# The low parts of the experts' weights made on VectorE alone, instead of on VectorE and GpSimd, in a decoder layer with 32 experts

## The chip, the cores and the metric

The kernel runs on one core of one Trainium2 chip. The metric is the time of one execution on the device in microseconds (us). Engines are named as the profile names them: PE is TensorE's matmul and PEld its weight load, DVE is VectorE, ACT is ScalarE, POOL is GpSimd, SP is SyncE, which here only issues transfers.

## What is computed

One decoder layer over 1024 tokens of width 1024 in float32: a mixer of three branches, a layer norm, then a mixture of experts, and a second layer norm. The change lies in the mixture of experts. Each token takes its 4 best of 32 experts:

```
gu   = x @ w_gu[e] + b_gu[e]                 # 1024 -> 512, gate and up
act  = (clip(up, -7, 7) + 1) * (min(gate, 7) * sigmoid(1.702 * min(gate, 7)))
y   += weight * (act @ w_down[e] + b_down[e])   # 256 -> 1024
```

An expert's weights come as six tiles of 128 x 1024 numbers, 512 KB each: four of `w_gu` (two row blocks of 128 in each) and two of `w_down`.

## The kernel before, in words

**Three products for one.** PE multiplies in a rounded form of float32. To keep the accuracy, every operand is split in two: the high part is a copy in the rounded form (made on ACT), the low part is what the copy lost, operand minus high part (a subtract, `tensor_tensor`, on DVE or POOL). Each product is then three matmuls: high by high, high by low, low by high (`mm3`, lines 221 to 224). `split` (line 217) makes both parts; for the `w_gu` tiles `expert_split` (line 1216) does, with the copy at line 1223 and the subtract at line 1226.

**The experts' loop** (lines 1658 to 1717) goes over 46 blocks of at most 128 rows each. `PLAN` gives each of 32 slots a number of rows; the fullest expert has four blocks, eleven slots have two, twenty have one, the last four of these 64 rows. `ORDER` puts a slot with two blocks between two with one block from the fourth slot on: a triple of three experts has four blocks. In one turn of the loop, for block b, the engines are given in this order: a gather of the rows of block b + 3 (an indirect DMA, issued by POOL, line 1282), the gate-up product of block b in three pieces (`gu_mm`), between them the transposes of block b + 1 (`x_T`) and of the activations of block b - 1 (`act_T`), the activation of block b (`swiglu`, DVE and ACT), the down product of block b - 1 (`down`, whose results DVE scales into the tile `o` at line 1482), and a scatter that adds block b - 2 into the output (an indirect DMA, issued by POOL, line 1488). Each engine works off its own instructions in the order in which they are written.

**The next expert's weights.** While an expert's blocks run, the six weight tiles of the next expert are split. `expert_units` (line 1230) makes six small functions, and `pump` calls them at three places of a turn: after the first third of `gu_mm`, after its last third, and after `down`. With one block in the expert that runs, each place takes two of the six; with two blocks, one. Which engine makes a low part stands in the tuple `engs`, one entry per tile, four for `w_gu` and two for `w_down`. The tuple that is used depends on the blocks of the expert whose weights are split.

**The loads.** The raw tiles lie in a ring of nine places (`mring`). SP issues the six loads of an expert (lines 830 and 833), three experts ahead in the program, but a load waits until the low part of the tile that had its place is made (`mring.give`, line 1227). SP's queue is in order: one load that waits holds all behind it, among them the small loads of the row tables (`table_load`, line 1265), which the gathers wait for.

**Ahead of the loop** the first two experts' weights are split under tuples of their own (line 1252). The second one's four `w_gu` tiles are split by hand (lines 1604 to 1632: two low parts on DVE, two on POOL), so only its last two entries, for `w_down`, are read from its tuple (line 1655).

Of the kernel before, what the change touches and what calls it, by code (L numbers as in the profile page):

```python
# [144 lines left out]
def body(ctx, tc, A, out, offs, dbg=None):  # L145
    nc = tc.nc
    V, G, SC, PE, SY = nc.vector, nc.gpsimd, nc.scalar, nc.tensor, nc.sync
# [51 lines left out]
    def slot(kind, shape, dt=F32):  # L199
        n = turn[kind] = turn.get(kind, -1) + 1  # L200
        tag = SLOTS[kind][n % len(SLOTS[kind])]
        full = [shape[0], 2048 if tag[0] == "r" else 1024] if kind in ("x", "o", "xT", "gu") else None
        pool = keep if kind == "tt" else bigp if tag == "big" else mb[0] if kind in ("sg", "up", "gs") or tag[:2] == "dn" else ph
        if full and len(shape) > 2:
            full = [shape[0], shape[1], full[1] // shape[1]]
        return pool.tile(shape, dt, tag=tag, name=kind, bufs=COUNT.get(tag, 1), padded_shape=full)
# [10 lines left out]
    def split(src, hi, lo, eng=V):  # L217
        SC.copy(hi, src)  # L218
        eng.tensor_tensor(lo, src, hi.bitcast(F32), op=ALU.subtract)  # L219
# [983 lines left out]
    nblk = [-(-n // P) for n in PLAN]  # L1203
# [8 lines left out]
    def expert_loads(s):  # L1212
        for q in range(6):
            mring.add(expert_load(s, q), (s, q))

    def expert_split(s, q):
        r = mring.take((s, q))
        hi_, lo_ = slot("gu", [P, D], F32R), slot("gu", [P, D], F32R)
        for k in range(2):
            ew[s]["gu"][2 * q + k] = (hi_[:, half_of(k)], lo_[:, half_of(k)])  # L1220

        def hi():
            SC.copy(hi_, r)  # L1223

        def lo(eng=V):
            eng.tensor_tensor(lo_, r, hi_.bitcast(F32), op=ALU.subtract)  # L1226
            mring.give((s, q))
        return hi, lo

    def expert_units(s, engs=None):  # L1230
        engs = engs or ((V, V, V, G, G, G) if nblk[s] > 1 else (V, V, V, G, V, G))
        def gu_unit(q):
            def f():
                hi, lo = expert_split(s, q)
                hi()
                lo(engs[q])
            return f

        def dn_unit(k):
            def f():  # L1240
                r = mring.take((s, 4 + k))
                w = slot("dn", [P, 2, D], F32R)
                split(r, w[:, 0, :], w[:, 1, :], engs[4 + k])
                mring.give((s, 4 + k))
                ew[s]["dn"][k] = w
            return f
        return [gu_unit(q) for q in range(4)] + [dn_unit(k) for k in range(2)]

    e0, e1, e2, e3 = order[:4]
    for s in (e0, e1, e2, e3):  # L1250
        expert_loads(s)
    units = [expert_units(e0, (V, V, V, G, V, V)), expert_units(e1, (V, V, G, G, G, G))]

    bgu = slot("bgu", [2 * E, 2 * F], F32R)
    bgf = slot("bgu", [2 * E, 2 * F])
# [402 lines left out]
    for b in range(2, NB + 1):  # L1658
        if b < NB:
            s, i = blocks[b]  # L1660
            if b in (3, 4, 5):
                ovl = next(ovl_steps)
            if b == 5 or b > 5 and i == 0:
                at = 1 if b == 5 else order.index(s)
                for f in pend:
                    f()
                pend = []
                if at > 1 and at + 3 < NS:
                    table_load(order[at + 3])
                    expert_loads(order[at + 3])  # L1670
                if at + 1 < NS:
                    pend = expert_units(order[at + 1])
# [174 lines left out]
```

## Time and profile before

| what | value |
|---|---|
| median of 3 runs | 1115.52 us (1114.58 to 1115.7) |
| the profiled execution | 1116.49 us |
| its span, first to last instruction | 1114.5 us |
| PE busy | 975.9 us, 88% of the span |
| ACT busy | 490.5 us, 44% |
| mean granted clock of TensorE | 0.948 |
| moved by DMA | 219.20 MB, 197 GB/s over the span |

The span is 2 us shorter than the profiled execution's own time, which is 1 us above the median of the other runs. A share of busy time is an average over stages; the experts' loop is a stretch of some 480 us of the span. A granted clock of 1.00 is 2.4 GHz throughout a stretch; 0.91 means that part of it ran at the lower level, 1.2 GHz.

### The profile page before, as it was taken

The page shows a single profiled execution, that of the slowest core. Times are in us where ns is not written, and L with a number is a line of the kernel's source. Part 1 is how long each engine was busy: PE and PEld are TensorE (multiplying, and loading weights), DVE is VectorE, ACT ScalarE, POOL GpSimd, SP SyncE. Part 2 cuts the span into 40 slices and gives each one's busy share as a digit, 9 for nine tenths or more (in the row PEclk, how much of TensorE's full clock was granted, in tenths as well). Part 3 has the DMA queues.
Part 4 walks back from the last instruction along what each step waited for, and adds up shares of the span by engine and source line. Part 5 has one row for each costly group of instructions (what it writes and reads, how often), then busy time and mean ns, then how long its engine had stood idle before and what let it go on. Part 6 is the DMA issues. An engine that isn't in the chain of part 4 may idle for free. (4 is left out here: it accounts for less than half of the span.)

```text
span 1114.5 us, 14260 instructions
## 1 busy us (share of the span) xinstructions
PE 975.9 (88%) x4538; PEld 748.3 (67%) x4538; DVE 852.6 (77%) x1400; ACT 490.5 (44%) x790; POOL 529.3 (47%) x327
## 2 busy tenths in 40 slices
PE   5899999999999988799779999998878989898730
PEld 4678779788887767678657777776655666565420
DVE  5737577836687896577686889998867999989948
ACT  2353132312454443234542546555444664564525
POOL 2540011011001155666682677676575876858633
PEclk9999999999999999799899999999998999999875
DMA  9902247435341236025748899998979899979745
GB/s 311 330 17 78 74 135 225 146 127 192 111 139 48 78 113 200 38 100 172 256 178 226 248 276 317 296 259 250 261 211 289 239 300 280 276 229 297 220 118 207
DMA packets 115652, 219.20 MB, mean 197 GB/s; under 512 B 21166, under 2 KB 42680, under 8 KB 115576
## 3 DMA queue, kind: packets, MB, share of 16 engines
q1 hardware_dynamic: 99416, 181.50, 48.8%
q0 software_dynamic: 16160, 36.78, 14.7%
q8 instruction: 36, 0.59, 0.2%
q14 instruction: 40, 0.33, 0.1%
HBM read 187.27 MB, written 36.78 MB: 201 GB/s over the span
## 5 line engine op out<-in xcount | busy, mean ns | idle before, releaser
L1226 DVE TENSOR_TENSOR gu<-raw,gu 128x1024 fp32r<-128x1024 f32 x95 | 216.8, 2298 | 18.8 <-ACT gu L1223 18.7
L1223 ACT CAST gu<-raw 128x1024 fp32r<-128x1024 f32 x128 | 130.4, 1048 | 47.0 <-DMA raw<-in_w_gu 46.3
L1488 POOL DMA_INDIRECT y_d<-o,tt x46 | 92.3, 2007 | 99.3 <-DVE aT L219 21.2
L223 PE MATMUL bank<-gu,xT 128*128 128x512 f32 (+10 forms) x280 | 111.2, 397 | 12.2 <-POOL gu L1226 10.0
L222 PE MATMUL bank<-gu,xT 128*128 128x512 f32 (+10 forms) x280 | 120.1, 429 | 0.0
L219 POOL TENSOR_TENSOR dn<-raw,dn 128x1024 fp32r<-128x1024 f32 x42 | 116.0, 2899 | 0.5 <-ACT dn L218 0.4
L224 PE MATMUL bank<-gu,xT 128*128 128x512 f32 (+10 forms) x280 | 111.3, 398 | 0.0
L224 PE MATMUL bank<-dn,aT 128*128 128x512 f32 (+11 forms) x184 | 77.8, 423 | 23.3 <-DVE aT L219 23.2
L1282 POOL DMA_INDIRECT x<-h_d,tt x46 | 70.9, 1540 | 53.3 <-DMA raw<-in_w_down 22.1
L1226 POOL TENSOR_TENSOR gu<-raw,gu 128x1024 fp32r<-128x1024 f32 x33 | 81.9, 2483 | 17.5 <-ACT gu L1223 16.9
L222 PE MATMUL bank<-u,w 128*128 128x512 f32 x216 | 86.6, 401 | 0.0
L223 PE MATMUL bank<-u,w 128*128 128x512 f32 x216 | 84.8, 393 | 0.3 <-DVE u L219 0.3
L224 PE MATMUL bank<-u,w 128*128 128x512 f32 x216 | 84.8, 392 | 0.0
L218 ACT CAST dn<-raw 128x1024 fp32r<-128x1024 f32 x64 | 65.3, 1046 | 43.1 <-PE bank L224 24.7
L218 ACT CAST xT<-bank 128x512 fp32r<-128x512 f32 (+11 forms) x92 | 46.4, 507 | 77.0 <-PE bank L1394 73.8
L222 PE MATMUL bank<-w,u 128*128 128x512 f32 (+1 forms) x192 | 76.0, 396 | 3.0 <-ACT u L379 3.0
L222 PE MATMUL bank<-dn,aT 128*128 128x512 f32 (+11 forms) x184 | 77.3, 420 | 0.5 <-ACT aT L218 0.4
L223 PE MATMUL bank<-dn,aT 128*128 128x512 f32 (+11 forms) x184 | 76.5, 416 | 0.0
L335 DVE SCALAR_TENSOR_TENSOR acc<-raw,cact,acc 128x512 f32<-128x512 f32 x80 | 68.0, 850 | 7.7 <-DMA raw<-in_w_ada 5.8
L224 PE MATMUL bank<-w,u 128*128 128x512 f32 (+1 forms) x192 | 70.7, 368 | 2.5 <-POOL u L380 2.4
L1482 DVE SCALAR_TENSOR_TENSOR o<-bank,tt,u 128x512 f32<-128x512 f32 (+11 forms) x92 | 65.4, 740 | 8.1 <-PE bank L224 7.5
L223 PE MATMUL bank<-w,u 128*128 128x512 f32 (+1 forms) x192 | 70.3, 366 | 1.1 <-DVE w L219 1.1
(417 smaller groups left out, 2298.4 us busy)
## 6 DMA issues: line engine op xcount, KB each, us to landing
raw<-in_w_gu SPq DMA_DIRECT2D x128, 512.0 KB
raw<-in_w_down SPq DMA_DIRECT2D x64, 512.0 KB
raw<-in_w_ada SPq DMA_DIRECT2D x32, 512.0 KB
raw<-in_w_ada SPq DMA_DIRECT2D x32, 256.0 KB
raw<-in_w_in SPq DMA_DIRECT2D x12, 512.0 KB
raw<-in_w_out SPq DMA_DIRECT2D x8, 512.0 KB
raw<-in_x SPq DMA_DIRECT2D x8, 512.0 KB
h_d<-h SPq DMA_DIRECT2D x8, 512.0 KB
```

Source lines behind the costliest of these rows:

```text
L218: SC.copy(hi, src)
L219: eng.tensor_tensor(lo, src, hi.bitcast(F32), op=ALU.subtract)
L222: PE.matmul(o, lh, rh, start=first, stop=False)
L223: PE.matmul(o, lh, rl, start=False, stop=False)
L224: PE.matmul(o, ll, rh, start=False, stop=last)
L335: V.scalar_tensor_tensor(acc, w[:, k, :], cact[:, kk:kk + 1], acc, op0=ALU.mult, op1=ALU.add)
L1223: SC.copy(hi_, r)
L1226: eng.tensor_tensor(lo_, r, hi_.bitcast(F32), op=ALU.subtract)
L1282: G.indirect_dma_start(out=x[:n], out_offset=None, in_=src, in_offset=bass.IndirectOffsetOnAxis(ap=segs[blocks[b]][:n, 0:1], axis=0), boun ...
L1482: V.scalar_tensor_tensor(o[:n, half_of(hf)], p_[:n], segs[s, i].bitcast(F32)[:n, 1:2], G2[:n, half_of(hf)], op0=ALU.mult, op1=ALU.mult)
L1488: G.indirect_dma_start(out=y_d, out_offset=bass.IndirectOffsetOnAxis(ap=segs[blocks[b]][:n, 0:1], axis=0), in_=outs.pop(b)[:n], in_offset= ...
```

## The change

Two tuples are replaced. In the loop every one of the six low parts of an expert is now made on DVE; before, POOL made three of six for experts with two blocks and two of six for those with one. Ahead of the loop the two `w_down` tiles of the second expert move to DVE as well. The first expert's tuple keeps one POOL entry, and the two subtracts of lines 1631 and 1632 stay on POOL.

```diff
     def expert_units(s, engs=None):
-        engs = engs or ((V, V, V, G, G, G) if nblk[s] > 1 else (V, V, V, G, V, G))
+        engs = engs or (V,) * 6
...
-    units = [expert_units(e0, (V, V, V, G, V, V)), expert_units(e1, (V, V, G, G, G, G))]
+    units = [expert_units(e0, (V, V, V, G, V, V)), expert_units(e1, (V, V, G, G, V, V))]
```

## Rows read from the trace of the kernel before

**Rows 1.** Page, part 1; groups by line, whole span (busy us, mean ns | idle).
```profile
PE 975.9 (88%) x4538; PEld 748.3 (67%) x4538; DVE 852.6 (77%) x1400; ACT 490.5 (44%) x790; POOL 529.3 (47%) x327
...
L1226 DVE TENSOR_TENSOR gu<-raw,gu 128x1024 fp32r<-128x1024 f32 x95 | 216.8, 2298 | 18.8 <-ACT gu L1223 18.7
...
L219 DVE TENSOR_TENSOR dn<-raw,dn 128x1024 fp32r<-128x1024 f32 x22 | 38.2, 1739 | 2.6 <-ACT dn L218 2.6
```

**Rows 2.** Windows: us, PE PEld DVE ACT POOL busy (x), clock, DMA share, GB/s.
```profile
619.70:669.80 50.10, 47.72 (x227) 36.83 (x226) 43.04 (x48) 26.53 (x39) 35.70 (x18) 1.00 0.95 270
669.80:712.10 42.30, 40.32 (x190) 30.30 (x189) 39.34 (x44) 24.39 (x36) 32.19 (x15) 1.00 0.99 311
754.60:804.30 49.70, 43.78 (x188) 31.80 (x187) 40.88 (x46) 25.11 (x35) 31.60 (x15) 0.93 0.91 258
804.30:860.80 56.50, 44.35 (x188) 30.82 (x187) 38.85 (x42) 24.72 (x35) 35.26 (x17) 0.91 0.83 245
860.80:901.50 40.70, 38.22 (x172) 26.62 (x170) 38.84 (x45) 24.47 (x36) 27.19 (x13) 0.96 0.87 256
901.50:945.20 43.70, 40.37 (x182) 27.65 (x182) 41.79 (x45) 24.33 (x37) 32.00 (x16) 0.96 0.98 289
...
619.70:1032.70 413.00, 373.96 (x1679) 266.26 (x1678) 364.16 (x399) 222.44 (x318) 291.17 (x138) 0.96 0.92 269
```

**Rows 3.** The costliest groups of the loop, 619.7 to 1032.7 us: DVE, then POOL.
```profile
L1226 DVE TENSOR_TENSOR gu<-raw,gu 128x1024 fp32r<-128x1024 f32 x81 | 192.7, 2394 | 18.0 <-ACT gu L1223 17.9
...
L219 DVE TENSOR_TENSOR dn<-raw,dn 128x1024 fp32r<-128x1024 f32 x18 | 28.5, 1582 | 2.6 <-ACT dn L218 2.6
...
L219 POOL TENSOR_TENSOR dn<-raw,dn 128x1024 fp32r<-128x1024 f32 x37 | 102.9, 2935 | 0.0
...
L1226 POOL TENSOR_TENSOR gu<-raw,gu 128x1024 fp32r<-128x1024 f32 x27 | 66.6, 2465 | 8.4 <-ACT gu L1223 7.8
```

**Rows 4.** Lines 1226 and 219, whole span: ns min/median/max, first and last start.
```profile
L1226 DVE TENSOR_TENSOR gu<-raw,gu x95: 1201/1223/6476, 502.1 to 1053.7; 128x1024 fp32r<-128x1024 f32 x95
...
L219 DVE TENSOR_TENSOR dn<-raw,dn x22: 1206/1225/4207, 559.7 to 1059.8; 128x1024 fp32r<-128x1024 f32 x22
```

**Rows 5.** Timeline at 876 us: start us, us, engine line, operation.
```profile
876.36 2.96 POOL L219 TENSOR_TENSOR dn<-raw,dn 128x1024 fp32r<-128x1024 f32 x1
...
876.82 3.59 DVE L1226 TENSOR_TENSOR gu<-raw,gu 128x1024 fp32r<-128x1024 f32 x1
```

**Rows 6.** Waits, 619.7 to 1032.7 us: who <- for whom: us, times, longest.
```profile
ACT gu L1223 <- DMA raw<-in_w_gu: 42.2, 28, 5.6
PE bank L224 <- DVE aT L219: 17.9, 10, 5.1
PE bank L223 <- POOL gu L1226: 10.0, 3, 5.0
...
SPq L830 <- POOL dn L219: 139.7, 37, 10.3
SPq L830 <- POOL gu L1226: 58.5, 18, 12.0
```

**Rows 7.** Timeline at 746 to 764 us: ACT, POOL, SP's queue, PE [idle before <-releaser].
```profile
746.16 1.04 ACT L1223 CAST gu<-raw 128x1024 fp32r<-128x1024 f32 x1 [4.18 <-DMA raw<-in_w_gu]
...
760.60 1.05 POOL L1282 DMA_INDIRECT x<-h_d,tt  x1 [7.75 <-PE bank L1394]
761.68 2.35 POOL L1226 TENSOR_TENSOR gu<-raw,gu 128x1024 fp32r<-128x1024 f32 x1
...
764.06 5.35 SPq L830 DMA_DIRECT2D raw<-in_w_gu  x3
...
764.09 0.50 PE L223 MATMUL bank<-gu,xT 128*124 128x512 f32 x1 [2.96 <-POOL gu L1226]
```

**Rows 8.** Lines 1282 (gathers) and 1488 (scatters): ns min/median/max, first and last start.
```profile
L1282 POOL DMA_INDIRECT x<-h_d,tt x46: 995/1800/2169, 536.3 to 1030.1; - x46
...
L1488 POOL DMA_INDIRECT y_d<-o,tt x46: 1417/1831/5019, 591.9 to 1073.0; - x46
```

## The prediction, made before the changed kernel was run

> **What bounds the kernel now.** I read the page first, for the shares: PE is busiest, DVE next, POOL under half [rows 1]. These are averages, so I cut the experts' loop into stretches by the copy that opens every third expert, from the fourth on; each stretch holds a triple of experts [rows 2]. Between the second and third shown lies one of 42.5 us, much like the second; after the last shown follow two of 43.8 and 43.7. The first stretch works off five blocks, the other eight four each. See three things there. The stretch from 669.8 and the next are full: PE is busy 40.3 of 42.3 us and the transfers take 0.99 of their engines' time. The stretches from 754.6 and 804.3 take 49.7 and 56.5 us for the same work; in them PE idles 5.9 and 12.2 us, its granted clock falls to 0.93 and 0.91, and the transfers fall to 0.91 and 0.83. And over all nine PE idles 39 of 413 us. So PE and the weight loads set the pace where all goes well, and something breaks the flow elsewhere.
>
> Next, the costliest groups of the loop [rows 3]. A low part on DVE takes 2.39 us in the mean, but 1.22 us in the median and 1.20 at least [rows 4]. The timeline says where the rest comes from: DVE's subtract that starts at 876.82, while POOL's runs, ends 1.1 us after POOL's end at 879.32, as if it had begun only then [rows 5]. In the nine stretches 40 of DVE's 99 low parts took over 1.3 us; all 40 lie over a subtract of POOL's, and none of the 59 others took over 1.23 us, though 29 of them lie over a gather or a scatter and no subtract of POOL's. So DVE's busy time holds much standing still behind POOL's subtracts.
>
> Last, the waits [rows 6]. SP's load issues wait 139.7 and 58.5 us for low parts made on POOL; ACT's copies wait 42.2 us for weights that have not landed; PE waits 17.9 us for the low part of the activations (DVE) and 10.0 us for POOL's `w_gu` parts. One place shows how they hang together [rows 7]: a tile's copy ends at 747.2, but POOL stands in a gather that waits 7.75 us for PE's transposes, so the low part runs from 761.68 to 764.03, 14.5 us late. At 764.06 SP can issue the next loads, and at 764.09 PE goes on.
>
> **The change, part by part.**
>
> Moved in the nine stretches: 37 and 27 subtracts, 64, leave POOL [rows 3]; at the median of 1.223 us they add 64 x 1.223 = 78.3 us to DVE. What DVE loses is its standing still: 81 x (2.394 - 1.223) = 94.9 us and 18 x (1.582 - 1.225) = 6.4 us, together 101.3. So DVE goes from 364.2 us to 341, or 37.9 a stretch, against 42.3 in the best full stretch. That leaves room, if not much. If none of the stall were POOL's doing, DVE would need 364.2 + 78.3 = 442.5; these are the two ends. I take the lower one, since all 40 long cases lie over POOL's subtracts.
>
> POOL loses 102.9 + 66.6 = 169.5 us and keeps the gathers and scatters. These now come earlier and meet more subtracts of DVE's. A gather took 1.0 us at least and 1.8 in the median, a scatter 1.4 and 1.8 [rows 8]. Nearest price of meeting one: up to the 0.8 us between a gather's ends; for 74 of them 59 us at most on an engine with 291 - 169 = 122 us of work in 413. Nothing, covered by POOL's idle time; without that cover a gather is 0.8 us late, three blocks before PE needs it.
>
> SP's loads no longer pass POOL's queue. They wait for DVE's low part instead, which stands in DVE's order one place behind the copy of its tile. For the case of rows 7 that would be some 1.3 us after the copy's end, not 14.5. Behind a waiting load stand the row tables that gathers need, so they gain too.
>
> A new wait: DVE's queue now holds the low parts of `w_down` in front of the next turn's transposes and activations. They follow ACT's copy, 1.04 us as in [rows 7], which must follow PE's down product. ACT is ahead of DVE in most turns, and a subtract that waits costs at most that copy. I cost it in the first rival.
>
> One rule of the Trainium skill speaks against the change. Perfetto Trace Analysis, Optimizing Scalar/DVE Operations, says that when DVE is saturated, work may be worth giving to ScalarE or even GPSIMD, with the reserve that GPSIMD shares an SBUF port with DVE. By the first half alone the loop's DVE, 364 of 413 us busy, should get slower by what it is given back; by the reserve the busy time is partly POOL's. The trace agrees with the reserve: 101 us of stall against 78 of work.
>
> **The sum.** What stall goes, the loads and PE are next: even without it no stretch runs faster than PE's work, and the loads at 0.99 as in the best stretch need 0.92 x 413 / 0.99 = 384 us for all nine. So I let each four-block stretch run like the best full ones, at 42.4: 49.7 gives 7.3, 56.5 gives 14.1, the three of 43.7 to 43.8 give 1.3 each (4.0). The five-block one (PE idle 2.4 of 50.1), the two full ones and that of 40.7 I leave. Together 25.4, so 413 becomes 388, close to the 384 of the loads. Outside the nine stretches eight more subtracts move: 8 x 1.22 = 9.8 us more work. The stall there is the whole span's less the nine stretches': 95 x 1.075 - 94.9 = 7.2 us for `w_gu` [rows 1], by the same step 4.9 for `w_down` (22 with a mean of 1.739 [rows 1]). The net is 2.3 less, nearly all in the last experts; I take 2. The sum is 27.4. The profiled execution took 1116.5 (span 1114.5 and 2 around it), so 1089.1; it lies 1.0 above the median, so 1088.
>
> **The rivals.**
>
> DVE becomes the bound in the one-block turns. DVE's 341 us less 163 low parts x 1.223 leave 142 us for 37 blocks, 3.8 each. A one-block turn needs 6 x 1.22 + 3.8 = 11.2 us of DVE against 374 / 37 = 10.1 of PE. For it: two such turns follow each other in each triple. Against it: the two-block expert has 5 us to catch up in, and PE's need of DVE has some us of slack. If all of it lands on PE, 18 x 1.1 = 20 us, and with the copy's 1.04 in half of these turns 9 more, the time is 1108 to 1117; half of it is likelier, near 1100.
>
> PE never waits. Its idle 39 us go and the clock stays at 1.00: the nine take some 370, so 1116.5 - 43 - 2 - 1 = 1070. For it: the stretch at 40.7 had transfers at only 0.87. Against it: the loads' 384.
>
> Nothing moves: the loads set the pace by bytes, at 269 GB/s in the mean as now, and 1115 stays. Against it the 311 GB/s of one stretch.
>
> Slower: the stall is not POOL's subtracts' but comes from something that stays, such as the weights' own landing. Then DVE needs the 442 us, 29 more than the nine stretches take, and the time is 1145. It decides once more than 68 of the 101 us of stall stay (341 + 68 is about the present 413). Against it stand the 40 of 40.
>
> That the change does not do what it says can be left out: only three subtracts of weights stay on POOL, all ahead of the loop.
>
> **How the numbers follow.** A measurement of this kernel tells 0.2%, 2.2 us, from no change. Forecast (1080 to 1097) 0.58; DVE as the bound (to 1112) 0.17; PE alone (1066 to 1080) 0.11; nothing moves 0.06; slower 0.08. So faster 0.86, same 0.06, slower 0.08. The likeliest time is 1088; for 8 in 10 the range takes in the forecast and most of its two neighbours, 1068 to 1110.
>
> **What would show it.** Right: DVE's mean for line 1226 falls from 2.4 to about 1.23 us in the loop, with nearly twice the count; DVE's busy time there falls slightly; POOL has gathers and scatters alone; SP's waits name DVE and shrink from 10 us apiece to a few; no stretch of four blocks is over 45 us and the clock there stays over 0.95; the transfers' share is near 0.97. Wrong: DVE's subtracts still at 2 us (the slower rival), PE waiting longer for the activations' low part with DVE over 95% busy (the first), or transfers at 0.99 and stretches no shorter.

## The result, and the profile of the changed kernel

The changed kernel takes 1083.91 us in the median of four runs (1080.66 to 1096.13), the kernel before 1115.61 in four on the same chip. The ratio is 0.973, 95% interval 0.970 to 0.977: 2.7% faster. The prediction was 1088, from 1068 to 1110. The profiled execution took 1084.64 us, its span is 1082.8. On the page (part 1, busy us, share of the span, instructions) POOL has lost 72 subtracts and DVE has gained them, yet DVE is busy 35 us less:

```profile
PE 967.5 (89%) x4538; PEld 748.2 (69%) x4538; DVE 817.6 (76%) x1472; ACT 489.0 (45%) x790; POOL 363.9 (34%) x255
```

The same nine stretches as in [rows 2], in the changed kernel (us, PE PEld DVE ACT POOL busy, clock, DMA share, GB/s), and all nine together:

```profile
618.70:665.80 47.10, 47.10 (x227) 36.96 (x226) 41.49 (x57) 26.47 (x39) 15.55 (x10) 1.00 0.98 313
665.80:705.50 39.70, 39.70 (x190) 30.41 (x189) 36.97 (x51) 24.40 (x35) 11.95 (x8) 1.00 1.02 328
705.50:745.20 39.70, 39.70 (x190) 30.12 (x189) 36.50 (x50) 24.43 (x35) 14.84 (x8) 1.00 1.00 290
745.20:794.30 49.10, 42.58 (x187) 31.51 (x185) 37.69 (x53) 24.69 (x36) 16.93 (x9) 0.93 0.97 281
794.30:836.20 41.90, 39.52 (x183) 27.84 (x183) 37.02 (x52) 24.62 (x37) 12.93 (x7) 1.00 0.93 285
836.20:879.90 43.70, 40.40 (x181) 28.02 (x182) 36.94 (x52) 24.32 (x37) 15.39 (x9) 0.96 0.92 279
879.90:924.80 44.90, 39.99 (x180) 28.08 (x180) 36.38 (x52) 24.17 (x36) 25.53 (x9) 0.92 0.96 281
924.80:963.40 38.60, 38.41 (x182) 26.07 (x181) 36.14 (x52) 23.84 (x36) 17.43 (x8) 1.00 0.98 294
963.40:1001.40 38.00, 36.97 (x174) 24.42 (x173) 36.24 (x53) 24.10 (x37) 11.71 (x7) 1.00 0.98 310
...
618.70:1001.40 382.70, 364.38 (x1682) 263.42 (x1680) 335.37 (x464) 221.04 (x318) 142.27 (x73) 0.98 0.97 295
```

They take 382.7 us where they took 413.0, so 30.3 of the span's 31.7 us come from here. Five stretches have PE busy for the whole of their length or all but 1 us of it, among them the two that were full before: 42.3 and 42.5 us became 39.7. The one of 56.5 us, the worst, now takes 41.9. Two are still long: 49.1 us, with PE idle for 6.5 us and a granted clock of 0.93, and 44.9 at 0.92.

The costliest groups over the nine, of DVE and then of POOL, which answer to [rows 3]:

```profile
L1226 DVE TENSOR_TENSOR gu<-raw,gu 128x1024 fp32r<-128x1024 f32 x108 | 127.7, 1214 | 4.3 <-ACT gu L1223 3.7 <-DMA tt<-tab_d 0.3
L219 DVE TENSOR_TENSOR dn<-raw,dn 128x1024 fp32r<-128x1024 f32 x55 | 65.4, 1214 | 3.2 <-ACT dn L218 2.9 <-DMA raw<-in_w_down 0.3
...
L1488 POOL DMA_INDIRECT y_d<-o,tt x37 | 75.5, 2040 | 197.8 <-DVE xT L219 39.3 <-DMA y_d<-o,tt 37.5 <-DVE gu L1226 26.9
L1282 POOL DMA_INDIRECT x<-h_d,tt x36 | 68.0, 1890 | 47.3 <-PE bank L1394 14.9 <-DMA tt<-tab_d 12.9 <-DMA y_d<-o,tt 8.5
```

Low parts take 1.214 us in the mean, about the median before, 1.223 and 1.225 us [rows 4]. DVE's own busy time fell from 364 to 335 us although it makes 163 low parts in these stretches instead of 99. The waits (who <- for whom: us in total, times, longest), for [rows 6]:

```profile
PE bank L1394 <- DMA x<-h_d,tt: 17.2, 8, 6.1
ACT gu L1223 <- DMA raw<-in_w_gu: 4.7, 3, 2.6
PE bank L224 <- DVE aT L219: 1.0, 1, 1.0
```

And those of SP's queue:

```profile
SPq L830 <- DVE dn L219: 129.5, 49, 10.9
SPq L833 <- DVE gu L1226: 61.6, 31, 4.9
```

PE's waits for the low part of the activations fell from 17.9 to 1.0 us and those for POOL's parts are gone. ACT waits 4.7 us for weights instead of 42.2. A new wait has taken the first place: PE waits 17.2 us for gathered rows. In the kernel before, that was 4.6:

```profile
PE bank L1394 <- DMA x<-h_d,tt: 4.6, 2, 3.0
```

### The profile page after: what moved, and what is told of

Same layout as the page of the kernel before. It is cut to its first block, busy times and chain, and to the rows that moved or that the text cites. A ratio compares the mean times of both kernels' runs of the same rounds, so it can differ in the third digit from the quotient of the medians.

```text
span 1082.8 us, 14221 instructions
## 1 busy us (share of the span) xinstructions
PE 967.5 (89%) x4538; PEld 748.2 (69%) x4538; DVE 817.6 (76%) x1472; ACT 489.0 (45%) x790; POOL 363.9 (34%) x255
## 5 line engine op out<-in xcount | busy, mean ns | idle before, releaser
L1226 DVE TENSOR_TENSOR gu<-raw,gu 128x1024 fp32r<-128x1024 f32 x125 | 151.2, 1241 | 5.1 <-ACT gu L1223 4.5
L1282 POOL DMA_INDIRECT x<-h_d,tt x46 | 82.7, 1798 | 53.2 <-PE bank L1394 15.4
L222 PE MATMUL bank<-w,u 128*128 128x512 f32 (+1 forms) x192 | 76.7, 399 | 3.0 <-ACT u L379 3.0
L219 DVE TENSOR_TENSOR dn<-raw,dn 128x1024 fp32r<-128x1024 f32 x64 | 75.9, 1213 | 3.2 <-ACT dn L218 2.9
L1394 PE MATMUL bank<-ce,x 128*128 128x128 f32 (+11 forms) x368 | 52.6, 269 | 27.8 <-DMA x<-h_d,tt 24.3
L1482 DVE SCALAR_TENSOR_TENSOR o<-bank,tt,u 128x512 f32<-128x512 f32 (+11 forms) x92 | 65.5, 740 | 10.9 <-DMA y_d<-o,tt 6.4
L224 PE MATMUL bank<-dn,aT 128*128 128x512 f32 (+11 forms) x184 | 72.5, 394 | 1.2 <-DVE aT L219 1.2
L222 PE MATMUL bank<-dn,aT 128*128 128x512 f32 (+11 forms) x184 | 72.8, 396 | 0.4 <-ACT aT L218 0.4
L219 DVE TENSOR_TENSOR xT<-bank,xT 128x512 fp32r<-128x512 f32 (+11 forms) x92 | 53.6, 585 | 25.1 <-ACT xT L218 24.8
L224 PE MATMUL bank<-w,u 128*128 128x512 f32 (+1 forms) x192 | 71.0, 370 | 1.6 <-POOL u L380 1.6
L223 PE MATMUL bank<-dn,aT 128*128 128x512 f32 (+11 forms) x184 | 72.3, 393 | 0.0
```

The source lines that it names most:

```text
L222: PE.matmul(o, lh, rh, start=first, stop=False)
L223: PE.matmul(o, lh, rl, start=False, stop=False)
L224: PE.matmul(o, ll, rh, start=False, stop=last)
L1282: G.indirect_dma_start(out=x[:n], out_offset=None, in_=src, in_offset=bass.IndirectOffsetOnAxis(ap=segs[blocks[b]][:n, 0:1], axis=0), boun ...
L1394: PE.transpose(p_[:, j * n:j * n + n], x[:n, blk(hf * 4 + j)], ident[:n, :n])
L1482: V.scalar_tensor_tensor(o[:n, half_of(hf)], p_[:n], segs[s, i].bitcast(F32)[:n, 1:2], G2[:n, half_of(hf)], op0=ALU.mult, op1=ALU.mult)
```

## The experiments

Two theories were tested first. **Stall**: POOL's subtracts hold DVE's up, and what DVE does next is late, above all the low part of the activations that PE waits for. **Queue**: low parts made on POOL are late because POOL's queue stands in a gather or scatter, as in [rows 7], and the loads and PE are late after them. Runs on other chips are compared by their ratio to the kernel before on the same chip (1119.7 to 1122.3 us in the median there).

**Idle subtracts back on POOL.** They are at the places where POOL made low parts; all low parts stay on DVE.

```diff
+        idle = () if engs else (3, 4, 5) if nblk[s] > 1 else (3, 5)
...
+        def extra(q):
+            if q in idle:
+                for h in range(2):
+                    scr = mb[0].tile([P, 512], F32, tag="scr", name="scr")
+                    G.tensor_tensor(scr, G2[:, half_of(h)], G2[:, half_of(h)], op=ALU.subtract)
...
                 lo(engs[q])
+                extra(q)
...
                 split(r, w[:, 0, :], w[:, 1, :], engs[4 + k])
+                extra(4 + k)
```

> The changed kernel, with POOL given idle subtracts again: wherever POOL made a low part in the loop before, it now subtracts one constant tile from itself into a scratch tile, in two halves of 512 columns, and nobody reads the result. All low parts stay on DVE. Theory 'stall' (POOL's subtracts hold up DVE's): the stall of about 100 us in the nine stretches comes back on top of DVE's 337 us, so DVE needs about 440 us where the stretches now take 383; DVE's mean for a low part goes from 1.21 to 1.8 us or more and the time to 1115 to 1145. Theory 'queue' (before, POOL's low parts were late because they stood behind gathers and scatters in POOL's queue): nothing waits for these subtracts, so the time stays within 1084 to 1092.

Measured: ratio 1.006 (1.002 to 1.011). The whole gain is gone, though nobody reads what POOL makes. The groups of DVE and POOL in the nine stretches, 412.8 us (in this run and the next, line numbers after the edit are ten higher):

```profile
L1226 DVE TENSOR_TENSOR gu<-raw,gu 128x1024 fp32r<-128x1024 f32 x108 | 162.3, 1534 | 2.2 <-ACT gu L1223 2.2
L219 DVE TENSOR_TENSOR dn<-raw,dn 128x1024 fp32r<-128x1024 f32 x55 | 86.6, 1599 | 2.2 <-ACT dn L218 1.9 <-DMA raw<-in_w_down 0.3
...
L1238 POOL TENSOR_TENSOR scr<-u 128x512 f32<-128x512 f32 x125 | 219.1, 1753 | 6.5
```

PE's waits there (who <- for whom: us in total, times, longest):

```profile
PE bank L224 <- DVE aT L219: 27.1, 15, 5.9
PE bank L1404 <- DMA x<-h_d,tt: 13.2, 8, 3.4
```

DVE's low parts are at 1.53 and 1.60 us: a stall of 54 us, about half of before. The forecasts of 1.8 us, and of 440 us of DVE's work, were too high: DVE is busy for 388 us. The time went all the same, since the stall lies where it hurts: PE's wait for the low part of the activations, 1.0 us in the changed kernel, is 27.1. ACT's copies wait for no weights in these stretches, so the stall does this without late loads.

**The same, without reads.** POOL fills the scratch tile with zeros instead, five times 512 columns at each place.

```diff
...
+                for h in range(5):
+                    scr = mb[0].tile([P, 512], F32, tag="scr", name="scr")
+                    G.memset(scr, 0.0)
...
```

> The counterpart of the run with idle subtracts on POOL: at the same places POOL fills the scratch tile of 512 columns five times with zeros, which reads nothing, so POOL's queue is held up about as long, but without a read. 'Stall by the subtracts' reads': DVE's low parts stay at 1.21 us in the mean and the ratio to the kernel before stays at 0.97 to 0.98 (some us for gathers and scatters that come later). If what made the idle subtracts dear was POOL's queue being held up, the ratio goes to 1.00 as there.

Measured: 0.978 (0.970 to 0.985). The groups of DVE and POOL in the nine stretches, 393.6 us:

```profile
L1226 DVE TENSOR_TENSOR gu<-raw,gu 128x1024 fp32r<-128x1024 f32 x108 | 127.7, 1215 | 3.2 <-ACT gu L1223 2.9 <-issue 0.2
...
L1238 POOL MEMSET scr<- 128x512 f32 x312 | 179.1, 574 | 15.0
```

PE's waits there (who <- for whom: us in total, times, longest):

```profile
PE bank L1404 <- DMA x<-h_d,tt: 25.5, 11, 8.9
PE bank L224 <- DVE aT L219: 1.0, 1, 1.0
```

POOL is held up for 179 us, against 219 by the idle subtracts and 170 by the real ones [rows 3], and DVE does not notice: 1.215 us. What may be lost against the changed kernel goes with PE's longer waits for gathered rows, 25.5 us instead of 17.2; with the idle subtracts these were shorter, 13.2, so they are not what made that run slow. So it is the reading POOL instruction that stalls DVE, and this stall is enough to undo the change; a POOL queue that is held up, with nothing waiting for what it makes, is worth a small part of it at most.

**Half of the change each.** First only `w_gu` moves, then only `w_down`.

```diff
-        engs = engs or ((V, V, V, G, G, G) if nblk[s] > 1 else (V, V, V, G, V, G))
+        engs = engs or ((V, V, V, V, G, G) if nblk[s] > 1 else (V, V, V, V, V, G))
```
```diff
-        engs = engs or ((V, V, V, G, G, G) if nblk[s] > 1 else (V, V, V, G, V, G))
+        engs = engs or (V, V, V, G, V, V)
```

> Half of the change: in the loop only the w_gu low parts move to DVE, the w_down ones stay on POOL as before (37 in the nine stretches). 'Stall': the gain goes by the number of subtracts taken from POOL, 27 of 64, so 0.42 of 31.7 us, about 1102. 'Queue': PE waited 10.0 us for POOL's w_gu parts and never long for its w_down parts, so nearly the whole gain is here, about 1088.

> The other half: in the loop only the w_down low parts move to DVE, one w_gu part of each expert stays on POOL (27 in the nine stretches). 'Stall': 37 of 64, so 0.58 of 31.7 us, about 1097. 'Queue' by PE's waits: little gain, 1108 to 1115, since PE still waits for the w_gu parts; by SP's waits (139.7 us for w_down parts against 58.5 for w_gu parts) seven tenths of the gain, 1093.

Measured: 0.990 (0.983 to 0.997) and 0.973 (0.965 to 0.982). With `w_gu` alone moved, DVE's low parts:

```profile
L1226 DVE TENSOR_TENSOR gu<-raw,gu 128x1024 fp32r<-128x1024 f32 x108 | 171.0, 1612 | 31.0 <-ACT gu L1223 30.5
L219 DVE TENSOR_TENSOR dn<-raw,dn 128x1024 fp32r<-128x1024 f32 x18 | 31.2, 1734 | 3.3 <-ACT dn L218 3.0 <-DMA raw<-in_w_down 0.3
```

PE's longest wait there (who <- for whom: us in total, times, longest):

```profile
PE bank L224 <- DVE aT L219: 27.6, 12, 6.2
```

With `w_down` alone moved, the same groups:

```profile
L1226 DVE TENSOR_TENSOR gu<-raw,gu 128x1024 fp32r<-128x1024 f32 x81 | 102.3, 1279 | 3.8 <-ACT gu L1223 3.4 <-DMA tt<-tab_d 0.3
L219 DVE TENSOR_TENSOR dn<-raw,dn 128x1024 fp32r<-128x1024 f32 x55 | 79.8, 1475 | 3.5 <-ACT dn L218 3.5
```

PE's waits there (who <- for whom: us in total, times, longest):

```profile
PE bank L1394 <- DMA x<-h_d,tt: 11.7, 7, 4.4
PE bank L223 <- POOL gu L1226: 6.9, 3, 3.0
PE bank L1450 <- POOL gu L1226: 4.1, 1, 4.1
PE bank L224 <- DVE aT L219: 1.4, 2, 1.2
```

And SP's wait for POOL's parts there:

```profile
SPq L830 <- POOL gu L1226: 126.7, 25, 13.9
```

The first half gives what the count of subtracts said. The second gives more than its 0.58: as far as can be told, the whole. The subtracts are not alike. The 37 that stay in the first half leave a stall of 108 x (1.612 - 1.223) + 18 x (1.734 - 1.225) = 51 us, 1.4 us each; the 27 in the second leave 81 x 0.056 + 55 x 0.250 = 18 us, 0.7 each. By stall instead of count, the shares of the 101 us taken away are 0.49 and 0.82. And POOL's `w_down` subtracts stand just ahead of the next turn's transposes and activations: with them PE waits 27.6 us for the activations' low part, without them 1.4.

For the `w_gu` parts Queue loses: with these left on POOL, PE still waits 6.9 and 4.1 us for them, about as long as in the kernel before [rows 6], SP's loads still wait 126.7 us for them, and the time is, as far as can be told, as good as with the whole change. It is not shown that those waits cost nothing, since PE's wait for rows is shorter in that run.

For the `w_down` parts the two theories cannot be told apart here. With these left on POOL, ACT waits for weights as it did before, and the longest of PE's waits came about like this (start us, us, engine line):

```profile
ACT gu L1223 <- DMA raw<-in_w_gu: 52.6, 25, 5.4
...
877.90 6.75 DVE L1226 TENSOR_TENSOR gu<-raw,gu 128x1024 fp32r<-128x1024 f32 x1 [2.80 <-ACT gu L1223]
878.44 5.12 POOL L219 TENSOR_TENSOR dn<-raw,dn 128x1024 fp32r<-128x1024 f32 x2
885.32 0.76 PE L224 MATMUL bank<-dn,aT 128*104 128x512 f32 x1 [6.18 <-DVE aT L219]
```

DVE idles 2.80 us for a copy that waited for its weights. Then one low part takes 6.75 us, over two of POOL's subtracts that had stood in its queue behind a scatter, which had waited 5.06 us for the one before it to land. PE's three next longest waits there, of 3.5 to 5.2 us, have the same before them: 2.9 to 4.8 us of idling, then a low part of 4.1 to 5.8 us. In the kernel before, the longest (5.1 us) has it too. So the run with idle subtracts shows that the stall alone is enough to lose the gain, but the kernel before had late loads as well, and how its loss divides between the two is not shown.

**Idle subtracts on DVE.** Two of 512 columns at the end of each turn of the changed kernel.

```diff
             pump(1 if per < 6 else 2)
+            for h in range(2):
+                scr = mb[0].tile([P, 512], F32, tag="scr", name="scr")
+                V.tensor_tensor(scr, G2[:, half_of(h)], G2[:, half_of(h)], op=ALU.subtract)
```

> The changed kernel with two idle subtracts of 512 columns on DVE at the end of every turn (about 1.3 us a turn, some 50 us in the nine stretches, on top of 335 of 383). The first rival of the prediction (DVE is the bound after the change): the whole 50 us come on top, ratio 1.01 or more. 'DVE has room, PE and the gathers bound it': less than 20 us, ratio 0.975 to 0.99.

Measured: 0.974 (0.967 to 0.981), no slower than can be told from the changed kernel. The added group:

```profile
L1708 DVE TENSOR_TENSOR scr<-u 128x512 f32<-128x512 f32 x74 | 50.8, 687 | 1.3
```

The nine stretches as one window (us, PE PEld DVE ACT POOL busy, clock, DMA share, GB/s):

```profile
620.60:1010.70 390.10, 367.56 (x1682) 260.92 (x1680) 377.60 (x538) 221.19 (x319) 115.90 (x72) 0.98 0.97 288
```

PE's waits there (who <- for whom: us in total, times, longest):

```profile
PE bank L224 <- DVE aT L219: 17.0, 20, 3.6
PE bank L1394 <- DMA x<-h_d,tt: 5.4, 2, 2.8
```

DVE is busy 378 of 390 us, 42 more than in the changed kernel, and the nine stretches grow by 7. PE waits longer for DVE (17.0 us), and less for rows (5.4 instead of 17.2): the delay mostly takes the place of another. DVE was not the bound.

**The new wait, for gathered rows.** One gather and PE's wait for its rows in the changed kernel:

```profile
769.00 1.35 POOL L1282 DMA_INDIRECT x<-h_d,tt  x1 [0.30 <-issue]
...
785.72 1.03 PE L1394 MATMUL bank<-ce,x 116*128 116x116 f32 x4 [6.06 <-DMA x<-h_d,tt]
```

The gather is issued by 770.4 us and PE goes on with its rows at 785.7, 15 us later; it would have taken them from 779.7. All gathers of the nine stretches, from the start of the issue to the landing:

```profile
DMA to landing us min/median/max: 6.2/8.9/18.1
```

Another gather was slow already in its issue:

```profile
901.15 5.33 POOL L1282 DMA_INDIRECT x<-h_d,tt  x1 [0.30 <-issue]
...
916.58 0.72 PE L1394 MATMUL bank<-ce,x 92*128 92x92 f32 x3 [4.84 <-DMA x<-h_d,tt]
```

The eight gathers of the nine stretches that no low part of DVE's lies over took 0.99 to 1.39 us, the eleven with over 2 us of low parts over them 1.94 to 6.16; before, none took over 2.17 [rows 8]. No run tests whether the low parts lengthen them.

Four edits asked why the rows are late. The first puts the gather ahead of the scatter in POOL's queue, the second loads the row tables one expert earlier, the third does both, and the fourth takes half the bytes of `w_down` away.

```diff
-            if b < NB - 3:
+            if b == 2:
                 gather(b + 3)
...
         down(b - 1)
+        if b < NB - 4:
+            gather(b + 4)
         if b > 2:
             scatter(b - 2)
```
```diff
-    for e in order[2:5]:
+    for e in order[2:6]:
         table_load(e)
...
-                if at > 1 and at + 3 < NS:
-                    table_load(order[at + 3])
+                if at > 1 and at + 4 < NS:
+                    table_load(order[at + 4])
+                if at > 1 and at + 3 < NS:
                     expert_loads(order[at + 3])
```
```diff
-                SY.dma_start(r, A["w_down"][e, blk(q - 4), :].rearrange("o p f -> p (o f)"))
+                SY.dma_start(r[:, :512], A["w_down"][e, blk(q - 4), :512].rearrange("o p f -> p (o f)"))
...
-                split(r, w[:, 0, :], w[:, 1, :], engs[4 + k])
+                for c in range(2):
+                    SC.copy(w[:, 0, half_of(c)], r[:, :512])
+                for c in range(2):
+                    engs[4 + k].tensor_tensor(w[:, 1, half_of(c)], r[:, :512], w[:, 0, half_of(c)].bitcast(F32), op=ALU.subtract)
```

> The changed kernel with the gather of block b + 4 issued after the down product of turn b, ahead of the scatter, instead of the gather of b + 3 at the top of turn b, behind the scatter. In the changed kernel PE waits 17.2 us in the nine stretches for gathered rows, and POOL's scatters wait 37.5 us for the scatter before to land. If the gathers are late because they stand behind such a scatter in POOL's queue, PE's waits for them go and the time falls by 10 to 20 us, to 1065 to 1075. If they are late because the transfers are full (share 0.93 to 1.02), it stays at 1082 to 1086.

Measured: 0.979 (0.971 to 0.986). PE waits for no rows in the nine stretches, but this came out otherwise than either theory had it; the longest waits of POOL's gathers, of DVE and of PE:

```profile
POOL x L1282 <- DMA tt<-tab_d: 53.6, 11, 11.0
...
DVE o L1482 <- DMA y_d<-o,tt: 35.4, 9, 10.9
...
PE bank L224 <- DVE aT L219: 28.0, 8, 11.6
```

The gathers, now first, wait for tables; the scatters behind them are late, DVE has no free tile `o`, and PE waits for the activations again.

> The changed kernel with each expert's row table loaded one expert earlier, so that it does not stand in SP's queue behind weight loads that wait for a place. In the changed kernel POOL's gathers wait 12.9 us for tables and PE 17.2 us for gathered rows. If the tables make the gathers late: POOL's waits for tables go and PE's waits for rows fall, ratio 0.965 or less. If the rows are late because they land slowly (15 us from issue in one case, where the transfers are full): no change, 0.973 give or take 0.005.

> The changed kernel with the row tables one expert earlier, once more, beside the changed kernel itself. If the tables were worth something, its ratio is below the changed kernel's by 0.005 or more (0.96 to 0.968); if 0.9644 was that chip's doing, the two agree within 0.003.

> The changed kernel once more, on the chip of the runs beside it, so that they can be compared with it directly. Ratio 0.97 to 0.977.

Measured: 0.964 (0.957 to 0.972), and once more beside the changed kernel itself: 0.966 (0.962 to 0.970) against that kernel's 0.971 (0.968 to 0.975; medians 1082.4 and 1086.4 us). With the tables early, no gather waits for a table any more in the second run, and PE's waits for rows stay (16.3 us in the changed kernel beside it):

```profile
PE bank L1394 <- DMA x<-h_d,tt: 15.8, 6, 8.9
```

So late tables are not what makes the rows late. The ratios differ by the 0.005 that was asked for, but their intervals overlap: a small gain, likely and not settled.

> Tables one expert earlier and the gather of b + 4 ahead of the scatter of turn b. With the gather ahead alone, PE did not wait for rows any more, but gathers waited 53.6 us for tables, held the scatters up behind them, and DVE waited 35.4 us for a free o tile. If that chain is right, the tables loaded earlier take DVE's wait for o away, and the time falls below the changed kernel's: ratio 0.955 to 0.968. If scatters are slow to land of themselves, DVE still waits 20 us or more for o and the ratio stays at 0.975 to 0.985.

Measured: 0.965 (0.957 to 0.972), likely better than the gather alone and no better than the tables alone. The ratio is that of the first theory, the wait that of the second: DVE still waits 20.7 us for `o` until scatters have landed, and PE 17.4 us for the activations. So late tables were part of that chain; whether the scatters that are left land slowly or are issued late is not shown.

> The changed kernel with half the bytes of w_down: only the first 512 of 1024 columns are loaded, and both halves of the split tile are made of them (so the down product uses wrong weights in its second half; all its operations stay, with the copies and subtracts of w_down in two pieces). A sixth of the weights' bytes goes. If PE waits for gathered rows because the transfers are full, these waits (17.2 us in the nine stretches) fall under 6 us, the share of the transfers under 0.9, and the ratio to 0.955 to 0.965. If the gathers are late through POOL's queue alone, PE's waits for rows stay above 12 us and the ratio at 0.97.

Measured: 0.955 (0.950 to 0.960). The nine stretches as one window (columns as above):

```profile
621.80:993.70 371.90, 361.38 (x1680) 262.38 (x1679) 338.22 (x520) 225.70 (x373) 140.11 (x72) 0.99 0.92 263
```

PE's waits there (who <- for whom: us in total, times, longest):

```profile
PE bank L1397 <- DMA x<-h_d,tt: 9.2, 6, 3.5
```

The gathers, from the start of the issue to the landing:

```profile
DMA to landing us min/median/max: 5.0/8.0/17.7
```

The waits for rows fall to 9.2 us, not under 6 as was said, with the transfers' share at 0.92, not under 0.9. (The line of the transposes is three higher here.) The ratio is in the range that was said, but fewer bytes help the weights too, so it does not tell the cause. The gathers land little sooner than in the changed kernel, 8.0 us against 8.9 in the median and 17.7 against 18.1 at most. So it is not shown that full transfers make them land late. Some gathers need 14 us and more at either share, and why is open.

**The part ahead of the loop.**

```diff
-    units = [expert_units(e0, (V, V, V, G, V, V)), expert_units(e1, (V, V, G, G, V, V))]
+    units = [expert_units(e0, (V, V, V, G, V, V)), expert_units(e1, (V, V, G, G, G, G))]
```

> The change in the loop alone: the second expert's tuple ahead of the loop stays as before, so its two w_down low parts are made on POOL. The prediction cost these two at next to nothing: the ratio is the changed kernel's within 0.004. If they held something up ahead of the loop, it is 0.005 or more above.

Measured: 0.972 (0.968 to 0.976), beside 0.971 for the whole change. These two subtracts are worth nothing that can be measured.

## Why the prediction was right, point by point

**The stall.** Right in its cause and its size: 101 us of DVE's busy time was standing still behind POOL's subtracts, and DVE went from 364 to 335 us where 341 was forecast. The experiments show it: idle subtracts on POOL undo the change, idle fills that hold POOL up for 179 us, about as long as its real subtracts did, do not. Late loads, the other part of the account [rows 7], went too: ACT's wait for `w_gu` tiles fell from 42.2 to 4.7 us. What each of the two gave is not shown. The Trainium skill's SBUF — State Buffer, Who interferes with whom, says that a DVE instruction with two SBUF inputs contends with a GpSimd instruction that reads SBUF, and not with one that only writes. These two runs agree: a low part took 1.53 us beside the subtracts, 1.215 beside the fills.

**The sum.** The total of 27.4 us was near the 31.7 measured between the two spans, but by two errors that partly cancel, so its closeness is in part luck. The step "even without it no stretch runs faster than PE's work, and the loads ... need 384 us" was wrong in its second half. The nine took 383 us, but at a share of 0.97, which is 371 us of transfer time where there were 380, for about the same bytes (295 GB/s for 383 us, 269 for 413); in one stretch the profile has the share at 1.02, at 328 GB/s. So the loads were no floor at 42 us, and the full stretches, which "I leave", fell to 39.7 us. This mis-sized term gave too little: the two full stretches and the five-block one gained 2.6, 2.8 and 3.0 us where nothing was forecast, and the last two, at 38.6 and 38.0 for 42.4, another 8.2. Against these 16.6 us, and 0.5 in the stretch at 794.3, stand three that ran worse than forecast: by 6.7 us at 745.2, 3.0 at 836.2 and 2.5 at 879.9. The net is the 4.9 us between 387.6 and 382.7.

The error on the other side is the step "Nothing, covered by POOL's idle time" for the gathers, with a cover of "three blocks". POOL was indeed idle enough: its gathers went from 1.64 to 1.89 us in the mean. But the price of "up to the 0.8 us" for a gather was too low, since single ones took up to 6.16 us. The cover is two turns, not three: the gather of block b + 3 is issued in turn b, and its rows are transposed in turn b + 2. And the landing, 8.9 us in the median and up to 18.1, was not priced. PE's waits for rows grew by 12.6 us, and 6.5, 3.3 and 4.8 us of them lie in the three stretches that ran worse, at 745.2, 836.2 and 879.9. **Outside the nine**, 2 us were forecast; they went from 701.5 to 700.1, so 1.4.

**A reading.** The low part in [rows 7] starts 14.5 us after its copy ends, and ends 16.8 us after it; the prediction sets 14.5 beside an end 1.3 us after the copy.

**The rivals.** DVE as the bound fell: 42 us more of DVE's busy time cost 7 us in the nine stretches. "PE never waits" came true in the five-block stretch and the two full ones, nearly in the last two, and not in the others. "Nothing moves" was wrong, since the nine stretches move 295 GB/s instead of 269, and so was the slower rival: no low part in them takes over 1.3 us any more.

**The signs.** Right: DVE's 1.21 us, its busy time slightly down, POOL with gathers and scatters alone, the transfers at 0.97. Wrong: "nearly twice the count" for line 1226 (95 became 125; it was the low parts of `w_down` that went from 22 to 64), SP's waits, whose "10 us apiece" had been the longest and not the usual (139.7 us in 37 is 3.8 apiece; now 129.5 in 49 is 2.6, and the longest still 10.9), and no four-block stretch over 45 us or under a clock of 0.95 (one at 49.1 and 0.93, one at 44.9 and 0.92).

**Work against stall.** What POOL took off DVE in work, 78 us, it more than gave back in stalls, 101 us, and the stalls came at bad moments. So of the Trainium skill's advice on a saturated DVE (Perfetto Trace Analysis, Optimizing Scalar/DVE Operations) the reserve, that an offload to GPSIMD might not help, is what this case's runs bear out.

## What to carry to other kernels

Compare an instruction's mean with its median on each engine before reading its busy time as work: a mean near twice the median, with the long cases all over one other engine's instructions, was standing still here. Here work on POOL that read a tile cost DVE 54 and 101 us of standing still, and work that only wrote one cost it nothing; so count the stall against the work moved, and weigh it by what DVE does next. When a stall goes, look for the wait that takes its place: here it is for gathered rows, whose landing the prediction had not priced.

## What was not expected of the hardware

A gather or scatter on POOL, whose row numbers lie in a tile of SBUF, never lengthened a subtract of DVE: in the changed kernel 82 of the 163 low parts in the nine stretches lie over one, and the longest of all takes 1.23 us. The other way round, a gather beside low parts took up to 6.16 us, where one without took at most 1.39. And an engine's added work can be free in time when another wait is in line: 42 us more busy DVE made the whole no slower than the runs can tell.
